# Routing cut in two: early token tiles are placed and gathered before the last tile is through its LayerNorm

## Chip, cores and metric

One core of one Trainium2 chip runs the whole program. The metric is the device time of one execution in microseconds (us). Five engines appear: TensorE (PE: matmuls; its weight loads are PEld), VectorE (DVE), ScalarE (ACT), GpSimd (POOL), and SyncE (SP), whose queue issues most transfers between HBM and the on-chip memory (SBUF).

## What is computed

A two-layer encoder on 512 tokens of width 1024. Layer 0 mixes tokens with a state-space part and gated linear attention, layer 1 with windowed attention; both end in a 1024x1024 output projection. Then a LayerNorm, a mixture of experts and a second LayerNorm:

```python
h = layer_norm(DEEPNORM_ALPHA * h + y, ln_mix_g[layer], ln_mix_b[layer])
y = hier_moe(h, ...)
h = layer_norm(DEEPNORM_ALPHA * h + y, ln_ffn_g[layer], ln_ffn_b[layer])

# hier_moe: xt is h as 512 rows
gp = softmax(xt @ w_group + b_group)              # 4 groups
grp = argmax(gp); p_grp = gp[tok, grp]
el = (xt @ w_router + b_router)[tok, grp]         # the 8 experts of that group
top_l, top_i = top_k(el, 2)
gate = softmax(top_l) * p_grp
# each of the two experts e of a token adds
#   gate * ((silu(x @ w1[e]) * (x @ w3[e])) @ w2[e])
```

There are 32 experts; w1 and w3 are 1024x512, w2 is 512x1024, all fp32.

## The kernel before

**Projection.** The 512 tokens are four tiles of 128. `out_part` makes one of four parts of a tile's output projection, each as three products (high and low halves of both operands). A tile is 48 matmuls of 512 columns; tile 3, the last, has 24 of 512 and 48 of 256 columns, which are as many columns in all. In layer 0 `out_proj` goes tile by tile: `operand(t)` transposes the mixer's output (tile `cat`) and splits it into `xh`, `xl`, four parts follow, and after them the tile's LayerNorm: `ln_stats` (L1067 to L1071; the power L1071 runs on POOL) and `ln_tile`, on DVE, with a row that multiplies by g (L1082) and a row that adds b (L1083), in two halves for tile 3. In layer 1 the same functions are called from `mixer1`, in an order written out by hand (`STEPS1`).

**Routing.** For each tile `route_tile` transposes x (L132, `ident`), copies it to `rxT` on ACT, multiplies it by the router's weights `wr` into the logits, and splits x into `xh` (ACT; DVE for tile 3) and `xl` (POOL, L1277). `logits` then adds the bias (L1282), and `route` does the rest for all four tiles at once: some 25 small DVE operations choose the group and the two experts, as a 0/1 matrix `ohb`; matmuls of `ohb` with the matrices `before` and `ones` give every token's place in its expert's list (`pos`); `select` compares it with a row of numbers to make the selection matrices `S`; `sort` ranks the experts by load (`eidx`, `erow`, `cap`); gates are worked out on DVE and POOL; `overflow_jobs` lists what doesn't fit; `gather` multiplies S by `xh` and `xl` (64 matmuls of 256 columns, 16 for a tile) and gives `xe`, the tokens in the experts' order; `arrange` brings places and gates into that order (`ppos`, `gT`, `gh`). Small matmuls called `warm` lie between, on the values as they come.

**Rounds.** `rounds` runs 13 rounds over the experts. `up` multiplies `xe` by w1 and w3, `turn` transposes, `down` multiplies by w2. SP streams weights into buffers of 2 MB (pools of 2, 2 and 3). Rounds 0 and 1 take fixed experts and are loaded ahead; later rounds are loaded by `eidx` (L1208).

**Who sets the order.** Inside `manual_schedule` PE keeps the order of the program; POOL's order follows the program everywhere; the rest is a scheduler's. Round 0 begins with the PE row `b<-w,xe` at L118.

Of the kernel before, what the change touches and what calls it, by code (L numbers as in the profile page):

```python
# [39 lines left out]
def row_bcast(ap1d, n, parts=128, off=0):  # L40
# [25 lines left out]
LP = 3  # L66

# [40 lines left out]
class Net:  # L108
# [862 lines left out]
    def mixer0_out(self, cat):  # L971
# [27 lines left out]
        def operand(t):  # L999
            for j in range(2):  # L1000
                b = self.bank()
# [44 lines left out]
    def out_proj(self, operand, hi, lo, split, layer, then, pre):  # L1046
# [4 lines left out]
        for t in range(4):  # L1051
            c = operand(t)
            for q in range(4):
                self.out_part(t, q, *c, hi, lo)
            self.ln_stats(t)
            self.ln_tile(t, gb)
            if t:
                then(t - 1)
        then(3)

    def ln_stats(self, t):
# [3 lines left out]
        if t == 3:  # L1065
            self.warm(st[:, 2, 0:1])
        V.bn_aggr(mv[:, 0:2], st.rearrange("p a b -> p (a b)"))  # L1067
        if t == 3:
            self.warm(mv[:, 0:1])
        V.tensor_scalar(mv[:, 2:3], mv[:, 1:2], 1e-5, None, op0=OP.add)  # L1070
        G.tensor_tensor(mv[:, 2:3], mv[:, 2:3], self.neghalf[:, 0:1], op=OP.pow)  # L1071
        if t == 3:
            self.warm(mv[:, 2:3])
# [178 lines left out]
    def route_tile(self, t):  # L1252

        nc = self.nc
        if t == 0:
            self.lgb = self.bank("l")
        V, S, G = nc.vector, nc.scalar, nc.gpsimd
        xT = []
        for j in range(2):
            b = self.bank("p")  # L1260
# [5 lines left out]
            if t == 3 and j == 0:  # L1266
                self.warm(x4[:, 0:1], 128)
            xT += [x4[:, 128 * k:128 * k + 128] for k in range(4)]
        hv = self.xh[:, t].rearrange("p k q -> p q k")
        if t == 3:  # L1270
            V.tensor_copy(hv, self.x[:, t].rearrange("p (q k) -> p q k", k=8))
        else:
            S.activation(hv, self.x[:, t].rearrange("p (q k) -> p q k", k=8), AF.Copy)
        lg = self.lgb[:, 36 * t:36 * t + 36]
        for k in range(8):
            self.mm(lg, xT[k], self.wr[:, k], k == 0, k == 7)
# [3 lines left out]
    def logits(self):  # L1280
        self.lg = self.M.tile([128, 4, 36], F32, name="lg", tag="lg")
        self.nc.vector.tensor_tensor(self.lg, self.lgb[:, 0:144].rearrange("p (t e) -> p t e", t=4),  # L1282
                                     self.br[:, None, :].to_broadcast([128, 4, 36]), op=OP.add)

    def route(self, layer):
        nc, M = self.nc, self.M
        V, S, G = nc.vector, nc.scalar, nc.gpsimd
# [4 lines left out]
        def rt(shape, name, dt=F32):  # L1292
            return M.tile([128] + shape, dt, name=name, tag=name)

        def bc(v, n):
            return v[:, :, None].to_broadcast([128, 4, n])
        lg = self.lg
        Gl, El = lg[:, :, 0:4], lg[:, :, 4:36]
        sm = rt([11, 4], "sm")
        gm, sg, pg, m1, m2, d21, den, g1, g2, kx, k2 = (sm[:, j] for j in range(11))  # L1300
        w4 = rt([3, 4, 4], "w4")
        ex, eq, ohg = (w4[:, j] for j in range(3))
        w8 = M.tile([128, 8, 4, 8], F32, name="w8", tag="hs", bufs=1)
        EM, key, oh1, oh2 = (w8[:, j] for j in range(4))
        w32 = w8[:, 4:8].rearrange("p a b e -> p (a b e)").rearrange("p (t g e) -> p t g e", t=4, g=4)
        gate = self.gate = rt([4, 32], "gate")

        def groups(v):

            return v[:, :, None].to_broadcast([128, 4, 4, 8]), ohg[:, :, :, None].to_broadcast([128, 4, 4, 8])  # L1310
        V.tensor_reduce(gm, Gl, axis=AX.X, op=OP.max)
        tt(eq, Gl, bc(gm, 4), OP.is_equal)
        tt(ex, Gl, bc(gm, 4), OP.subtract)
        tt(eq, eq, self.desc[:, None, 0:4].to_broadcast([128, 4, 4]), OP.mult)
        S.activation(ex, ex, AF.Exp)
        V.tensor_reduce(kx, eq, axis=AX.X, op=OP.max)
        tt(ohg, eq, bc(kx, 4), OP.is_equal)
        self.warm(gm[:, 0:1])
        self.warm(kx[:, 0:1])

        tt(w32, El.rearrange("p t (g e) -> p t g e", g=4), groups(EM)[1], OP.mult)
        V.tensor_reduce(EM, w32.rearrange("p t g e -> p t e g"), axis=AX.X, op=OP.add)
# [12 lines left out]
        tt(ohb.rearrange("p t (g e) -> p t g e", g=4), *groups(key), OP.mult)
        tt(d21, m2, m1, OP.subtract)

        b = self.bank()
        for t in range(4):
            o = b[:, 32 * t:32 * t + 32]  # L1340
            self.mm(o, self.before, ohb[:, t], True, t == 0)
            for s in range(t):
                self.mm(o, self.ones, ohb[:, s], False, s == t - 1)
        for t in range(4):
            self.mm(b[:, 128:160], self.ones, ohb[:, t], t == 0, t == 3)
        S.activation(d21, d21, AF.Exp)
        pos = self.pos = rt([4, 32], "pos")
        V.scalar_tensor_tensor(pos, b[:, 0:128].rearrange("p (t e) -> p t e", t=4), 1.0, ohb, op0=OP.add, op1=OP.mult)
        pb = self.bank()
        for t in range(4):  # L1350
            self.tp(pb[0:32, 128 * t:128 * t + 128], pos[:, t])
        self.posT = rt([512], "posT", BF)
        G.memset(self.posT, 0.0)
        cnt = self.cnt
        Sg = self.select(0, pos)
        V.tensor_scalar(self.posT[0:32], pb[0:32], 129.0, None, op0=OP.min)
        S.activation(cnt, b[:, 128:160], AF.Copy)
        self.sort(cnt)

        V.tensor_reduce(sg, ex, axis=AX.X, op=OP.add)  # L1360
# [5 lines left out]
        G.tensor_tensor(oh1, oh1, bc(g1, 8), op=OP.mult)  # L1366
        G.tensor_tensor(oh2, oh2, bc(g2, 8), op=OP.mult)
        G.tensor_tensor(oh1, oh1, oh2, op=OP.add)
        G.tensor_tensor(gate.rearrange("p t (g e) -> p t g e", g=4), *groups(oh1), op=OP.mult)
        self.overflow_jobs(layer, cnt)  # L1370
        xe = self.gather(0, Sg)
        self.arrange()
        if layer == 0:
            self.load_router(1)
        return xe, Sg

    def sort(self, cnt):
# [19 lines left out]
        b = self.bank()  # L1397
# [11 lines left out]

    def arrange(self):  # L1410
# [7 lines left out]
        b = self.bank()  # L1418
        for t in range(4):
            self.tp(b[0:32, 128 * t:128 * t + 128], self.gate[:, t])  # L1420
        gT = M.tile([128, 512], F32, name="gT", tag="GT", bufs=1)
        nc.scalar.activation(gT[0:32], b[0:32], AF.Copy)
        b = self.bank()
        for t in range(4):
            self.mm(b[:, 32 * t:32 * t + 32], gT[0:32, 128 * t:128 * t + 128], self.eone[0:32])
# [3 lines left out]
        nc.vector.tensor_tensor(self.gh[:, :, :, 1], bv, self.gh[:, :, :, 0].bitcast(F32), op=OP.subtract)  # L1429

    def select(self, g, pos=None):

        S = self.M.tile([128, 4, 256], F32R, name="S", tag="S", bufs=1)
        pos = self.ppos if pos is None else pos
        for kind, gr, q, p0 in ROUNDS:
# [4 lines left out]
            while a < len(ns):  # L1440
                m = sum(n == ns[a] for n in ns)
                d, o = [128, 4, m, ns[a]], 128 * q + sum(ns[:a])
                self.nc.vector.tensor_tensor(
                    S[:, :, o:o + m * ns[a]].rearrange("p t (a s) -> p t a s", a=m),
                    self.iota64[:, 0:ns[a]][:, None, None].to_broadcast(d),
                    pos[:, :, p0 + a:p0 + a + m][:, :, :, None].to_broadcast(d), op=OP.is_equal)
# [55 lines left out]
    def up(self, xe, q, ws, kind, between):  # L1502
# [3 lines left out]
        for b, nm in ((b1, "w1"), (b3, "w3")):  # L1506
            for k in range(8):
                for a, o, n in tiles(kind):
                    self.mm(b[o:o + n], xe[:, k, 128 * q + o:128 * q + o + n], ws[nm](a, k), k == 0, k == 7)
            if nm == "w1":  # L1510
# [59 lines left out]
    def moe(self, layer, then):  # L1570

        nx, S = self.route(layer)
        with self.tc.manual_schedule(engines={mybir.EngineType.PE}):
            parts = self.rounds(layer, nx, S)
# [519 lines left out]
```

## Time and profile before

| | us |
|---|---|
| median of 3 runs | 1565.31 |
| lowest and highest | 1565.18, 1565.65 |
| the profiled execution | 1567.3 |
| its span in the trace | 1565.5 |
| PE busy | 1395.2 (89%) |
| DVE busy | 672.0 (43%) |
| ACT busy | 370.4 (24%) |
| POOL busy | 138.6 (9%) |
| mean granted PE clock | 0.945 |

The span is what the trace covers of one execution; the 1.8 us between span and execution lie around it. Busy shares are means over a program with very different stages: two mixers, two routings (about 299 to 367 us and 1040 to 1081 us) and two runs of 13 rounds. PE streams matmuls one into the next, so the distance between two starts tells what one costs; the duration in a row also has its filling.

### The profile page before, as it was taken

The page shows a single profiled execution, that of the slowest core. Times are in us where ns is not written, and L with a number is a line of the kernel's source. Part 1 is how long each engine was busy: PE and PEld are TensorE (multiplying, and loading weights), DVE is VectorE, ACT ScalarE, POOL GpSimd, SP SyncE. Part 2 cuts the span into 40 slices and gives each one's busy share as a digit, 9 for nine tenths or more (in the row PEclk, how much of TensorE's full clock was granted, in tenths as well). Part 3 has the DMA queues.
Part 4 walks back from the last instruction along what each step waited for, and adds up shares of the span by engine and source line. Part 5 has one row for each costly group of instructions (what it writes and reads, how often), then busy time and mean ns, then how long its engine had stood idle before and what let it go on. Part 6 is the DMA issues. An engine that isn't in the chain of part 4 may idle for free. (4 is left out here: it accounts for less than half of the span.)

```text
span 1565.5 us, 21114 instructions
## 1 busy us (share of the span) xinstructions
PE 1395.2 (89%) x8299; PEld 817.3 (52%) x8299; DVE 672.0 (43%) x1467; ACT 370.4 (24%) x683; POOL 138.6 (9%) x120
## 2 busy tenths in 40 slices
PE   7998869989989999969797998998988999979885
PEld 6987656775525454324245865665434453424242
DVE  7989796462221332212127477663222223212125
ACT  3244735211101011001014565531101111101012
POOL 0000004230000000000005343021000000000003
PEclk9999889989999999999898999998999999999898
DMA  6233128365999999999995145475999999999993
GB/s 176 82 95 61 43 34 289 133 244 195 407 409 424 419 421 422 420 419 421 420 399 185 31 122 147 145 270 226 404 405 420 426 419 421 421 420 421 420 412 119
DMA packets 105879, 460.56 MB, mean 294 GB/s; under 512 B 17706, under 2 KB 43786, under 8 KB 63152
## 3 DMA queue, kind: packets, MB, share of 16 engines
q1 hardware_dynamic: 105664, 459.06, 75.0%
q8 instruction: 67, 1.10, 0.3%
q14 instruction: 36, 0.29, 0.1%
q0 software_dynamic: 112, 0.10, 0.0%
HBM read 454.41 MB, written 4.72 MB: 293 GB/s over the span
## 5 line engine op out<-in xcount | busy, mean ns | idle before, releaser
L118 PE MATMUL b<-w,xe 128*64 128x512 f32 (+1 forms) x2144 | 401.0, 618 | 37.9 <-DMA w<-in_moe_w_dram 34.5
L118 PEld LDWEIGHTS b<-w,xe 128*64 128x64 f32 (+1 forms) x2144 | 118.5, 127 | 289.5 <-issue 221.2
L118 PE MATMUL b<-w,hT 128*64 128x512 f32 (+1 forms) x1088 | 217.5, 629 | 33.8 <-DMA w<-in_moe_w_dram 30.9
L1567 DVE TENSOR_TENSOR x<-x,b 128x512 f32<-128x512 f32 x176 | 112.3, 682 | 156.5 <-PE b L118 154.2
L118 PEld LDWEIGHTS b<-w,hT 128*64 128x64 f32 (+1 forms) x1088 | 63.3, 129 | 173.7 <-issue 98.9
L1537 DVE SCALAR_TENSOR_TENSOR yl<-b,gs,yh 128x512 fp32r<-128x512 f32 x52 | 39.0, 751 | 215.2 <-ACT yh L1536 214.7
L118 PE MATMUL b<-S,xh 128*128 128x256 f32 x448 | 113.2, 293 | 0.0
L118 PE MATMUL b<-S,xl 128*128 128x256 f32 x448 | 111.5, 289 | 0.0
L1514 DVE TENSOR_TENSOR hs<-hs,b 128x512 f32<-128x512 f32 x26 | 17.9, 688 | 206.1 <-PE b L118 206.1
L118 PEld LDWEIGHTS b<-S,xh 128*128 128x128 f32 x448 | 88.7, 198 | 10.0 <-issue 9.9
L1536 ACT ACTIVATE yh<-b,gs 128x512 fp32r<-128x512 f32 x52 | 35.8, 688 | 234.2 <-PE b L118 233.9
L118 PE MATMUL b<-yh,GT 128*128 128x512 f32 x208 | 89.1, 432 | 0.1
L118 PEld LDWEIGHTS b<-S,xl 128*128 128x128 f32 x448 | 88.8, 198 | 0.0
L1100 POOL TENSOR_SCALAR lnmv<-lnmv 128x1 f32<-128x1 f32 x8 | 3.2, 398 | 963.9 <-DVE x L1099 483.9
L1522 ACT ACTIVATE hT<-b 128x512 f32<-128x512 f32 x26 | 15.6, 599 | 303.4 <-PE b L132 303.4
L118 PE MATMUL b<-yl,GT 128*128 128x512 f32 x208 | 81.9, 399 | 3.0 <-DVE yl L1537 3.0
L1513 ACT ACTIVATE hs<-b 128x512 f32<-128x512 f32 x26 | 15.6, 599 | 205.4 <-PE b L118 205.4
L118 PEld LDWEIGHTS b<-yh,GT 128*128 128x128 f32 x208 | 39.5, 190 | 46.3 <-issue 33.0
L118 PE MATMUL b<-wh,xt 128*128 128x256 f32 x384 | 54.6, 294 | 1.5 <-ACT wh L167 1.5
L1467 ACT ACTIVATE xe<-b 128x512 f32<-128x512 f32 (+1 forms) x56 | 31.7, 567 | 88.2 <-PE b L118 88.2
L118 PE MATMUL b<-xTh,spa 128*128 128x512 f32 x160 | 51.6, 394 | 0.5 <-ACT scv L1842 0.5
L118 PEld LDWEIGHTS b<-wh,xt 128*128 128x128 f32 x384 | 50.3, 199 | 2.7 <-ACT wh L167 1.9
(411 smaller groups left out, 2078.0 us busy)
## 6 DMA issues: line engine op xcount, KB each, us to landing
w<-in_moe_w_dram SPq DMA_DIRECT2D x288, 1024.0 KB, 19.8
w<-in_moe_w_dram SPq DMA_DIRECT2D x46, 2048.0 KB, 21.7
bias<-Ld SPq DMA_DIRECT2D x32, 384.0 KB, 3.5
wr<-in_ab_w_in_dram SPq DMA_DIRECT2D x8, 1024.0 KB, 5.8
x<-in_x_dram SPq DMA_DIRECT2D x8, 512.0 KB, 7.2
wo<-in_ab_w_out_dram SPq DMA_DIRECT2D x2, 2048.0 KB, 16.0
cw<-in_c_w_in_dram SPq DMA_DIRECT2D x2, 2048.0 KB, 11.4
cwo<-in_c_w_out_dram SPq DMA_DIRECT2D x16, 256.0 KB, 4.4
```

The costliest lines, as they stand in the source:

```text
L118: self.nc.tensor.matmul(o, l, r, start=start, stop=stop)
L1100: G.tensor_scalar(mv[:, 3:4], mv[:, 0:1], mv[:, 1:2], -1.0 / 1024, op0=OP.add, op1=OP.mult)
L1467: nc.scalar.activation(xe[:, 2 * kk:2 * kk + 2, 0:n], b.rearrange("p (j s) -> p j s", j=2)[:, :, 0:n], AF.Copy)
L1513: nc.scalar.activation(hs, b1, AF.Silu)
L1514: nc.vector.tensor_mul(hs, hs, b3)
L1522: self.nc.scalar.activation(hT, b.rearrange("p (k s) -> p k s", k=4), AF.Copy)
L1536: nc.scalar.activation(yh[:, j], b[j], AF.Copy, scale=gs)
L1537: nc.vector.scalar_tensor_tensor(yl[:, j], b[j], gs, yh[:, j].bitcast(F32), op0=OP.mult, op1=OP.subtract)
L1567: V.tensor_add(xs, xs, b)
```

## The change

- `route_tile` becomes `route_turn` (transposes, `rxT`, `xh`, now on ACT for every tile, and `xl`) and `route_logits`.
- `route` becomes `choose(a, z)`, `places(a, z)` and `gather_part(a, z)`, each for tiles a to z. With `CUT = 2, 3` layer 0 does tiles 0 and 1 first and layer 1 tiles 0 to 2; the rest comes after the last tile's logits. The sums of the two gathers stay in the same PSUM banks.
- `warm` goes from these places. `route_rest` has 16 matmuls of 512 columns that only fill (or start the banks at zero) while the last LayerNorm runs, and 6 more after the first gather.
- `sort`, `gates`, `overflow_jobs`, `gate_rows`, `pos_rows`, `arrange` and `slot_gates` go into round 0, behind parts of `up`.
- Layer 0's projection uses PSUM banks by tags (2, 2, 1, 2, 1) in place of eight free ones. In layer 1 the last three parts of the projection move from `STEPS1` into `mixer1_end`, in PE's written order, and `ln_mix`'s g and b are loaded a second time, into `w_yh`'s and `w_yl`'s places.

```diff
+CUT = 2, 3
+FILL, FILL2 = 3, 6
@@ def out_proj
-            if t:
-                then(t - 1)
-        then(3)
+            if t:
+                self.route_turn(t - 1)
+                self.route_logits(t - 1)
+        c = operand(3)
+        self.route_open()
+        with self.tc.manual_schedule(engines={mybir.EngineType.PE}):
+            if CUT[0] < 3:
+                self.choose(0, CUT[0])
+            self.out_part(3, 0, *c, hi, lo)
+            self.out_part(3, 1, *c, hi, lo)
+            self.route_turn(2)
+            self.out_part(3, 2, *c, hi, lo)
+            self.route_logits(2)
...
+            self.out_part(3, 3, *c, hi, lo)
+            self.route_rest(CUT[0], gb)
+
+    def route_rest(self, n, gb):
+
+        self.ln_stats(3)
+        self.ln_tile(3, gb)
+        self.gb0 = [self.bank("stst"[j]) for j in range(4)]
+
+        for _ in range(FILL):
+            for b in self.gb0:
+                self.mm(b, self.ones, self.posT)
+        for b in self.gb0:
+            self.mm(b, self.ones, self.posT, True, False)
+        self.route_turn(3)
+        self.places(0, n)
+        self.route_logits(3)
+        self.gather_part(0, n)
+        o = self.bank("o")
+        for _ in range(FILL2):
+            self.mm(o, self.ones, self.posT)
+        self.choose(n, 4)
+        self.places(n, 4)
+        self.gather_part(n, 4)
@@ def rounds
             def between():
                 steps(4)
+                if pr == 0:
+                    self.sort(self.cnt)
+                    self.gates()
+                    self.overflow_jobs(self.cnt)
+                    self.gate_rows()
                 GT.append(self.slot_rows(pr))
-            h = self.up(xe, q, W, kind, between)
+            h = self.up(xe, q, W, kind, between, self.pos_rows if pr == 0 else None)
+            if pr == 0:
+                self.arrange()
+            steps(2)
+            h = self.turn(h)
             if pr == 0:
                 gs = self.slot_gates(0, S)
-            steps(2)
-            h = self.turn(h)
@@ end of mixer1
+    def mixer1_end(self, hi, lo):
+
+        gb = self.load_gb("ln_mix", 1, self.rp, ("yh", "yl"))
+        self.load_round(1, 0)
+        self.route_open()
+        with self.tc.manual_schedule(engines={mybir.EngineType.PE}):
+            n = CUT[1]
+            self.route_turn(2)
+            self.out_part(3, 1, self.xh[:, 3], self.xl[:, 3], hi, lo)
+            self.route_logits(2)
+            self.choose(0, n)
+            self.out_part(3, 2, self.xh[:, 3], self.xl[:, 3], hi, lo)
+            self.out_part(3, 3, self.xh[:, 3], self.xl[:, 3], hi, lo)
+            self.route_rest(n, gb)
```

`order` rows below name a line, an instruction and its tiles; the changed kernel's L120 and L134 are L118 and L132 of before. First PE in layer 0, in the projection of tile 2 (`hi` and `lo` are the weights' halves), before:

```order
L118 MATMUL b_2893<-wr,rxT_2906 128x36 x4
L118 MATMUL b_2932<-hi_2693,xh 128x512
L118 MATMUL b_2959<-hi_2697,xh 128x512
L132 MATMUL b_2991<-ident,x 128x128 x4
L132 MATMUL b_2998<-ident,x 128x128 x4
L132 MATMUL b_3015<-ident,cat_1442 128x128 x4
L118 MATMUL b_2932<-hi_2693,xl 128x512
L118 MATMUL b_2932<-lo_2694,xh 128x512
```

and in the change, where this projection ends:

```order
L120 MATMUL b_2959<-lo_2698,xh 128x512
L134 MATMUL b_2991<-ident,x 128x128 x4
L134 MATMUL b_2998<-ident,x 128x128 x4
L134 MATMUL b_3015<-ident,cat_1442 128x128 x4
L134 MATMUL b_3022<-ident,cat_1443 128x128 x4
L120 MATMUL b_2893<-wr,rxT_2996 128x36 x4
```

The transposes of tile 1's x (`ident,x`) stood after the second matmul of tile 2's projection and now stand behind its last.

DVE in the LayerNorm of tile 1 at the same place, before:

```order
L1082 SCALAR_TENSOR_TENSOR x<-x,lnmv,ln_mix_g 128x1024
L1083 SCALAR_TENSOR_TENSOR x<-x,lnmv,ln_mix_b 128x1024
L1007 TENSOR_TENSOR xl<-b_2918,xh 128x512
L1007 TENSOR_TENSOR xl<-b_2925,xh 128x512
```

and in the change:

```order
L1114 SCALAR_TENSOR_TENSOR x<-x,lnmv,ln_mix_g 128x1024
L1009 TENSOR_TENSOR xl<-b_2918,xh 128x512
L1009 TENSOR_TENSOR xl<-b_2925,xh 128x512
L1115 SCALAR_TENSOR_TENSOR x<-x,lnmv,ln_mix_b 128x1024
```

The two halves of tile 2's `xl` moved ahead of the row that adds b.

PE at the start of round 0 in layer 0, in the change (before, the rows on `gate`, `gT` and `erow,posT` stood ahead of the first `w_0_0_0`):

```order
L120 MATMUL b_3362<-w_0_0_0_2729,xe_3038 64x512 x8
L134 MATMUL b_3372<-ident,pos 32x128 x4
L120 MATMUL b_3362<-w_0_0_1_2731,xe_3038 64x512 x8
L120 LDWEIGHTS rb
L120 MATMUL b_3399<-erow,rb 128x32
L120 LDWEIGHTS rb
L120 MATMUL b_3399<-identb,rb 128x32
L134 MATMUL b_3436<-ident,gate 32x128 x4
L120 LDWEIGHTS identb
L120 MATMUL b_3443<-posT,identb 64x512
```

The transposes of `pos` and `gate` and the matmuls of `sort` now lie between the products of w1.

## Rows read from the trace of the kernel before

**Rows 1.** Windows: span, its us; busy PE, PEld, DVE, ACT, POOL; PE clock; DMA share; GB/s.

```profile
371.00:825.00 454.00, 413.46 (x2326) 182.51 (x2324) 108.10 (x191) 49.20 (x77) 0.00 (x0) 0.98 1.01 414
...
352.00:371.00 19.00, 16.59 (x104) 13.31 (x106) 4.77 (x27) 3.27 (x6) 0.00 (x0) 0.82 0.04 5
...
388.00:390.00 2.00, 2.00 (x14) 0.59 (x10) 0.24 (x1) 0.00 (x0) 0.00 (x0) 1.00 0.66 238
```

**Rows 2.** Timeline (start, us, engine, line, count, [idle before]), round 0: PE and SP.

```profile
366.61 7.09 PE L118 MATMUL b<-w,xe 128*64 128x512 f32 x32
...
370.30 3.81 SPq L1222 DMA_DIRECT2D w<-in_moe_w_dram  x2
...
1081.38 7.09 PE L118 MATMUL b<-w,xe 128*64 128x512 f32 x32
```

**Rows 3.** Timeline of PE, layer 0, projections of tiles 2 and 3.

```profile
298.91 0.71 PE L118 MATMUL b<-hi,xh 128*128 128x512 f32 x2
302.63 1.97 PE L132 MATMUL b<-ident,x 128*128 128x128 f32 x8 [3.01 <-DVE x L1083]
...
317.20 1.87 PE L118 MATMUL b<-wr,rxT 128*128 128x36 f32 x16
...
319.30 0.47 PE L118 MATMUL b<-hi,xh 128*128 128x512 f32 x1
...
330.50 0.28 PE L118 MATMUL b<-lo,xh 128*128 128x256 f32 x1
```

**Rows 4.** Timeline of DVE and POOL, layer 0's LayerNorm rows.

```profile
287.79 1.28 DVE L1083 SCALAR_TENSOR_TENSOR x<-x,lnmv,ln_mix_b 128x1024 f32<-128x1024 f32 x1 [0.44 <-POOL lnmv L1071]
...
298.62 2.88 POOL L1277 TENSOR_TENSOR xl<-x,xh 128x1024 fp32r<-128x1024 f32 x1
...
298.69 3.89 DVE L1083 SCALAR_TENSOR_TENSOR x<-x,lnmv,ln_mix_b 128x1024 f32<-128x1024 f32 x1 [0.46 <-POOL lnmv L1071]
...
333.40 4.02 DVE L1083 SCALAR_TENSOR_TENSOR x<-x,lnmv,ln_mix_b 128x512 f32<-128x512 f32 x2
```

**Rows 5.** Timeline of ACT, DVE and PE, layer 0, from operands to round 0.

```profile
302.67 2.00 ACT L1273 ACTIVATE xh<-x 128x1024 fp32r<-128x1024 f32 x1 [3.72 <-DVE x L1083]
...
334.52 1.08 ACT L1265 ACTIVATE rxT<-b 128x512 f32<-128x512 f32 x2 [7.53 <-PE b L132]
...
343.87 0.31 DVE L1282 TENSOR_TENSOR lg<-b,br 128x144 f32<-128x144 f32 x1 [5.12 <-PE b L118]
...
349.08 0.29 DVE L1290 TENSOR_TENSOR ohb<-w,w 128x128 bf16<-128x128 f32 x1
...
350.53 1.29 DVE L1443 TENSOR_TENSOR S<-iota,pos 128x512 fp32r<-128x512 f32 x2
...
353.69 0.20 PE L118 MATMUL b<-erow,rb 32*128 32x32 bf16 x1 [2.52 <-DVE erow L1393]
...
354.44 0.41 PE L118 MATMUL b<-S,xh 128*128 128x256 f32 x1
...
359.35 0.41 PE L118 MATMUL b<-S,xl 128*128 128x256 f32 x1
...
360.09 0.28 PE L118 MATMUL b<-S,xh 128*128 128x256 f32 x1
...
364.17 0.27 PE L118 MATMUL b<-erow,posT 128*128 128x32 bf16 x4
...
365.60 1.07 PE L118 MATMUL b<-eone,gT 32*128 32x32 f32 x8 [0.73 <-ACT gT L1422]
```

**Rows 6.** Timeline of PE and DVE, layer 1, last parts of tile 3 and its LayerNorm.

```profile
1040.49 0.61 PE L118 MATMUL b<-chi,xh 128*128 128x512 f32 x2 [0.69 <-ACT xh L1961]
...
1047.91 0.28 PE L118 MATMUL b<-clo,xh 128*128 128x256 f32 x1
...
1050.81 4.00 DVE L1083 SCALAR_TENSOR_TENSOR x<-x,lnmv,ln_mix_b 128x512 f32<-128x512 f32 x2
```

**Rows 7.** Timeline of SP, layer 1: the weight load issued last before tile 3's parts.

```profile
1029.71 1.41 SPq L1222 DMA_DIRECT2D w<-in_moe_w_dram  x1
```

More of the change, by code (lines that the diff above doesn't have):

```diff
@@ L1044, in out_part, with out_proj @@
             V.bn_stats(self.lnst[:, t, j + (r if last else 0)], xs)
-    def out_proj(self, operand, hi, lo, split, layer, then, pre):
+    def out_proj(self, operand, hi, lo, split, layer, pre):
         split()
@@ L1050, in out_proj @@
         pre()
-        for t in range(4):
+        for t in range(3):
             c = operand(t)
@@ L1265, in route_tile @@
             S.activation(x4, b, AF.Copy)
-            if t == 3 and j == 0:
-                self.warm(x4[:, 0:1], 128)
-            xT += [x4[:, 128 * k:128 * k + 128] for k in range(4)]
+            self.rxT += [x4[:, 128 * k:128 * k + 128] for k in range(4)]
         hv = self.xh[:, t].rearrange("p k q -> p q k")
[L1270 to L1273, printed above, removed]
+        S.activation(hv, self.x[:, t].rearrange("p (q k) -> p q k", k=8), AF.Copy)
@@ L1280, in logits, with route_tile @@
[L1280 to L1287, printed above, removed]
+            self.mm(lg, self.rxT[k], self.wr[:, k], k == 0, k == 7)
+    def route_tile(self, t):
+        self.route_turn(t)
+        self.route_logits(t)
@@ new lines, in route_open, with rt @@
+    def route_open(self):
+        M = self.M
+        def rt(shape, name, dt=F32, **kw):
+            return M.tile([128] + shape, dt, name=name, tag=kw.pop("tag", name), **kw)
+        self.lg = rt([4, 36], "lg")
+        self.sm = rt([11, 4], "sm")
+        self.w4 = rt([3, 4, 4], "w4")
+        self.w8 = rt([8, 4, 8], "w8", tag="hs", bufs=1)
+        self.gate = rt([4, 32], "gate")
+        self.pos = rt([4, 32], "pos")
+        self.posT = rt([512], "posT", BF)
+        self.nc.gpsimd.memset(self.posT, 0.0)
+        self.S0 = rt([4, 256], "S", F32R, tag="S", bufs=1)
+        self.xe0 = self.half("xe0", [8, 256])
+        self.gb0 = []
@@ L1301, in route, with bc @@
[L1301 to L1310, printed above, removed]
+        def bc(v, m):
+            return v[:, :, None].to_broadcast([128, n, m])
@@ L1338, in route, with pos_rows @@
+    def pos_rows(self):
         b = self.bank()
         for t in range(4):
[L1340 to L1360, printed above, removed]
+            self.tp(b[0:32, 128 * t:128 * t + 128], self.pos[:, t])
@@ new lines, in pos_rows, with gates, tt @@
+        self.nc.vector.tensor_scalar(self.posT[0:32], b[0:32], 129.0, None, op0=OP.min)
+    def gates(self):
+        V, G = self.nc.vector, self.nc.gpsimd
+        def tt(o, x, y, op):
+            V.tensor_tensor(o, x, y, op=op)
+        gm, sg, pg, m1, m2, d21, den, g1, g2, kx, k2 = (self.sm[:, j] for j in range(11))
+        oh1, oh2 = (self.w8[:, j] for j in (2, 3))
+        bc = lambda v: v[:, :, None].to_broadcast([128, 4, 8])
+        V.tensor_reduce(sg, self.w4[:, 0], axis=AX.X, op=OP.add)
@@ L1365, in route, with gather_part @@
         tt(g2, g1, d21, OP.mult)
-        G.tensor_tensor(oh1, oh1, bc(g1, 8), op=OP.mult)
-        G.tensor_tensor(oh2, oh2, bc(g2, 8), op=OP.mult)
+        G.tensor_tensor(oh1, oh1, bc(g1), op=OP.mult)
+        G.tensor_tensor(oh2, oh2, bc(g2), op=OP.mult)
         G.tensor_tensor(oh1, oh1, oh2, op=OP.add)
[L1369 to L1375, printed above, removed]
+        G.tensor_tensor(self.gate.rearrange("p t (g e) -> p t g e", g=4), *self.groups(oh1), op=OP.mult)
+    def gather_part(self, a, z):
+        for t in range(a, z):
+            for k in range(8):
+                o = self.gb0[k // 2][:, 256 * (k % 2):256 * (k % 2) + 256]
+                self.mm(o, self.xh[:, t, k], self.S0[:, t], False, False)
+                self.mm(o, self.xl[:, t, k], self.S0[:, t], False, t == 3 and k % 2 == 1)
+                if t == 3 and k % 2:
+                    self.nc.scalar.activation(self.xe0[:, k - 1:k + 1], self.gb0[k // 2].rearrange("p (j s) -> p j s", j=2),
+                                              AF.Copy)
     def sort(self, cnt):
@@ L1500, in slot_rows, with up @@
         return GT
-    def up(self, xe, q, ws, kind, between):
+    def up(self, xe, q, ws, kind, between, within=None):
         nc = self.nc
@@ L1570, in moe @@
     def moe(self, layer, then):
-        nx, S = self.route(layer)
         with self.tc.manual_schedule(engines={mybir.EngineType.PE}):
-            parts = self.rounds(layer, nx, S)
+            parts = self.rounds(layer, self.xe0, self.S0)
+        if layer == 0:
+            self.load_router(1)
         with self.tc.issue_after(self.w2_dma.ins):
@@ L1619, in rounds, with overflow_jobs @@
         return parts
-    def overflow_jobs(self, layer, cnt):
+    def overflow_jobs(self, cnt):
         nc, M = self.nc, self.M
```

153 lines of the change are left out of this document (88 added, 65 removed), and 3 rows, old and new, of the table STEPS1.

## The prediction

> **What bounds the kernel now.** I read the windows first. Through the rounds of layer 0 (371 to 825 us) the DMA share is 1.01 at 414 GB/s while PE is busy 413 of 454 us: the stream of weights sets the pace [rows 1]. Just ahead, from 352 to 371, the DMA share is 0.04. So the rounds can't be shortened by what this change does, but they can be begun earlier. The timeline of PE and SP shows what begins them: round 0's first matmul starts at 366.61 in layer 0 and 1081.38 in layer 1, and the next weights are issued 3.7 us after the first, at 370.30, when w1's products have freed two buffers [rows 2]. The question for each layer is thus how much earlier round 0 starts, and what is added to round 0. The added work counts too: at 388 to 390 the stream has a gap again (share 0.66) [rows 1], because its next buffers wait for round 0's products, so PE still sets the pace there.
>
> The rest is two chains from projection to round 0, read row by row.
>
> **Layer 0, projection.** Tile 2's projection starts at 298.91. After two matmuls PE stands for 3.01 us because tile 1's x, which it is to transpose, isn't ready, and then works below full clock; it ends at 317.20 [rows 3], 18.3 us in all. Tile 3's projection, as many columns, takes from 319.30 to 330.78, that is 11.48 [rows 3]. In the change tile 1's transposes stand behind tile 2's projection, which then runs unbroken: 298.91 + 11.48 and 0.2 for its first products = 310.6. Behind it follow 8 transposes of x and 8 of the operand (1.0 each; the eight that were broken into took 1.97 below full clock [rows 3]) and the logits of tile 1, 1.87 [rows 3]: tile 3 starts at 314.5. Its own 11.48, with tile 2's transposes (1.0) and logits (1.87) woven in, ends at **328.9**, 1.9 before the old 330.8.
>
> **Layer 0, LayerNorm.** From the end of the projection to the last row on x (333.40 + 4.02 [rows 4]) it took 6.64. The row that adds b takes 1.28 when POOL is free and 3.89 when POOL's `xl` (2.88) runs beside it; that DVE row ended 1.1 us after POOL's [rows 4]. For tile 3 the two halves took 4.02 in the same way, where some 1.3 would be expected. In the change POOL's `xl` of tile 2 stands ahead of tile 3's power, and tile 2's x is ready long before, so nothing of POOL lies beside tile 3's rows: 6.64 - 2.6 = 4.0, x at 332.9. The bounds are 6.64 (the collision comes back) and 4.0. The 16 filling matmuls of 512 columns take 16 x 0.24 (twice the 0.12 below for 256 columns) = 3.8 at full clock and end within it.
> The Trainium skill says in "GPSIMD Engine Reference", section "8. Key points", that GpSimd shares its SBUF interfaces with VectorE and contends with DVE instructions that have two SBUF inputs; the row at 298.69 agrees, and by that rule the term is the same.
>
> **Layer 0, last logits and choice.** From x to the biased logits it took 6.4 (337.42 to 343.87 [rows 4, 5]). Now: `rxT` of the second half waits on ACT for `xh`, which moved there from DVE and takes 2.00; then 0.60 for that copy, half of 1.87 for the logits, and a few tenths for hand-overs [rows 3, 5]: I take 4.3, between 3.5 (the bare sum) and 6.4, nearest to the pieces since the small `warm` matmuls are gone. 337.2. The choice took 343.87 to 349.37, 5.5 [rows 5]. For two tiles the operations are as many and fixed costs rule them, so 5.5 again; POOL's `xl` of tile 3 now runs into it, for which I add 1.0 (bounds 0 and 2.6, the collision above): 343.7. Places and S took 2.45 after that (to 351.82 [rows 5]); for two tiles 2.0: 345.7. `sort` is no longer in the way, where PE waited 2.52 for `erow` [rows 5]. The last gather is 32 of 64 matmuls at 0.12 (34 starts from 360.09 to 364.17 [rows 5]) = 3.84; the first 32 and the 6 fillers lie beside the choice. Round 0 starts at **349.6** in place of 366.61, for `arrange` (364.17 to 366.61, 2.44 [rows 2, 5]) is also behind it now: **-17.0**.
>
> **Layer 1.** Here nothing is gained in the projection. PE went through tile 3's last parts from 1040.49 to 1048.19, 7.7 us [rows 6]. The logits of tile 2 (1.87) now stand between them, the parts are 72 pieces of 256 columns at 0.12 = 8.6, and I add 0.5 for the transposes: the end comes at 1051.5, **+3.3**. LayerNorm took 6.62 (to 1054.81 [rows 6]) with the same collision; 6.62 - 2.6 + 0.8, since tile 2's `xl` is now nearer = 4.8: 1056.3. Logits as above 4.3: 1060.6. The first gather is now 48 matmuls, 5.7, to 1066.3, and 6 fillers of 0.24 end at 1067.8, after the choice (1067.1). They and not the choice are late next here. Places and S 1.5, 16 matmuls 1.9: **1071.2** in place of 1081.38, **-10.2**.
>
> **Round 0.** `arrange`'s 2.44 and the four transposes of places (0.5) come into it, less the wait of 0.73 for `gT` [rows 5], which w3's products should cover: **+2.2** in each layer. Bounds: 0.5, if the stream and not PE sets round 0's pace after all (only the places' transposes lie ahead of the buffers that restart it), and 5, if each hand-over from DVE and POOL stops PE once more. `sort` and `gates` have 3.5 us of w1's products above them. Their late result, `eidx`, is first needed for the loads of round 2, which wait for round 1's buffers anyway: no cost. The second load of g and b adds 1 MB in layer 1, 2.5 us at 414 GB/s, ahead of an idle stream: no cost unless the gain there were above 10.
>
> **Sum.** -17.0 + 2.2 - 10.2 + 2.2 = -22.8. The profiled execution is 1567.3, so 1544.5; it lies 2.0 over the median of the runs, so the median becomes **1542.5**.
>
> **Rivals.**
> 1. *The clock falls and the gathers run at half of it.* In before the first 24 gather matmuls came every 0.2135 us (354.44 to 359.35), the later ones every 0.12 [rows 5], after PE had waited 2.52; the granted clock of that window is 0.82, a mix of the 1.2 and 2.4 GHz levels [rows 1]. The change leaves PE some 2 us without work while ACT copies `xh`. For it speaks that the wait of 3.01 was followed by slow transposes [rows 3]; against it the fillers. Price: layer 0's last 32 at 0.2135 cost +3.0; in layer 1 48 cost +4.5, the fillers +1.4, the last 16 +1.5. Together +10.4: **1552.9**. Half of it, when the clock comes back during the first gather, is as good as in my range. The Trainium skill, "TensorE: Matmul & The Clock Gate", section "What's actually happening", has the throttled state as the default, which activity releases; by it idle PE in these chains would bring this rival. The trace bears that out for the first gather of before.
> 2. *Round 0 hides what is moved into it.* The 1.01 share speaks for it, the gap at 388 against it [rows 1]. Then +0.5 in place of +2.2, 3.4 in all: **1539.1**.
> 3. *The change doesn't do what it says:* PE's written order in round 0 has `sort`'s matmuls and the transposes of `gate` among w1's and w3's products, so PE stands wherever DVE or POOL is late, and the tables cost there what they cost before. `sort` alone made PE wait 2.52, `gT` 0.73 [rows 5]; with the collisions of POOL and DVE on top, 5 to 11 in each layer is lost: **1553 to 1565**.
> 4. *Slower: layer 1's second load of g and b.* It stands on SP behind 5 MB of weights, the last of which is issued at 1029.71 [rows 7] and which take 12 us at 414 GB/s; it also waits for its place to be free. LayerNorm of tile 3 needs it at about 1053, so on paper it is early by some 8 us. Should the place be free only late, every weight behind it in the queue is late as well. It costs one for one from 1053 on and decides when it comes after 1053 + 22.8 = 1076; at 1083, **1572**. Nothing in the trace shows such a late reader, so the chance is small.
>
> **Chances.** Forecast 0.49, clock 0.30 (half or whole), round 0 hidden 0.11, not carried through 0.07, slower 0.03. The range 1537 to 1554 takes in the first three, with the collision terms' bounds; what is left out is most of rivals 3 and 4 and some mishap of the sum. A measurement of this kernel tells 0.2% (3.1 us) from nothing. Faster by more than that is the forecast, rivals 1 and 2 and most of 3: 0.92. Within it: the upper end of 3, 0.04. Slower 0.04.
>
> **What would show it.** Round 0's first matmul at 348 to 351 and at 1069 to 1073 (counted from the span's start); the projection of tile 2 in 11 to 12 us without a break; tile 3's two rows that add b at 0.7 each; gather starts 0.12 apart; the weights' stream restarting 4 us after round 0 starts. Gathers 0.21 apart mean rival 1. A distance between round 0 and round 1 that grew by under 1 means rival 2, by over 5 rival 3. A wait of DVE for `ln_mix` in layer 1 means rival 4. The sum is wrong if round 0 starts earlier by these amounts and the end doesn't follow.

## The result, and the profile after

The changed kernel takes **1543.2 us** (median of 4 runs, 1538.5 to 1547.2) where the kernel before, run beside it, takes 1565.5 (1565.2 to 1567.1): a ratio of 0.9854, 95% interval 0.9826 to 0.9883. Forecast were 1542.5, from 1537 to 1554. The same kernel in a second comparison gave 1540.7 and 0.9875 (0.9846 to 0.9905). Runs of one kernel differ by up to 1% there (before: 1553 to 1569), so stages are compared by their traces below.

The profiled execution of the changed kernel took 1547.2. First round 0 and the issue of weights behind it, the answer to [rows 2] (timeline, columns as there):

```profile
351.92 3.65 PE L120 MATMUL b<-w,xe 128*64 128x512 f32 x16 [0.72 <-ACT xe L1436]
...
355.62 4.50 SPq L1254 DMA_DIRECT2D w<-in_moe_w_dram  x2
...
1059.08 3.65 PE L120 MATMUL b<-w,xe 128*64 128x512 f32 x16 [0.72 <-ACT xe L1436]
```

Round 0 starts 14.7 us earlier in layer 0 and 22.3 earlier in layer 1, and the stream again restarts 3.7 after it. A wait shows that the prediction had not named: 0.72 for the last copy of `xe`.

The projections of layer 0, the answer to [rows 3], and the fillers behind them:

```profile
300.17 0.71 PE L120 MATMUL b<-hi,xh 128*128 128x512 f32 x2
...
311.20 1.04 PE L134 MATMUL b<-ident,x 128*128 128x128 f32 x8
...
314.65 0.47 PE L120 MATMUL b<-hi,xh 128*128 128x512 f32 x1
...
328.89 3.63 PE L120 MATMUL b<-posT,ones 128*128 128x512 bf16 x16
```

Tile 2's projection now takes 11.0 us without a break. Next DVE and POOL, the answer to [rows 4]:

```profile
299.88 1.28 DVE L1009 TENSOR_TENSOR xl<-b,xh 128x512 fp32r<-128x512 f32 x2
300.34 2.96 POOL L1301 TENSOR_TENSOR xl<-x,xh 128x1024 fp32r<-128x1024 f32 x1
301.07 3.31 DVE L1115 SCALAR_TENSOR_TENSOR x<-x,lnmv,ln_mix_b 128x1024 f32<-128x1024 f32 x1
...
331.66 1.41 DVE L1115 SCALAR_TENSOR_TENSOR x<-x,lnmv,ln_mix_b 128x512 f32<-128x512 f32 x2
...
335.74 2.86 POOL L1301 TENSOR_TENSOR xl<-x,xh 128x1024 fp32r<-128x1024 f32 x1 [4.25 <-ACT xh L1300]
```

Tile 3's two rows take 1.41 together in place of 4.02; tile 1's row is still held (3.31), but no longer stands ahead of tile 2's `xl`. Then the routing of layer 0, the answer to [rows 5], from ACT, DVE and PE:

```profile
333.71 1.96 ACT L1300 ACTIVATE xh<-x 128x1024 fp32r<-128x1024 f32 x1
335.47 0.62 ACT L1297 ACTIVATE rxT<-b 128x512 f32<-128x512 f32 x1
...
338.06 0.23 DVE L1338 TENSOR_TENSOR lg<-b,br 128x72 f32<-128x72 f32 x1 [3.16 <-PE b L120]
...
342.37 0.22 DVE L1338 TENSOR_TENSOR ohb<-w,w 128x64 bf16<-128x64 f32 x1
...
344.03 1.47 PE L120 MATMUL b<-posT,ones 128*128 128x512 bf16 x6
...
346.04 0.23 DVE L1397 SCALAR_TENSOR_TENSOR pos<-b,ohb 128x64 f32<-128x64 f32 x1 [3.37 <-ACT cnt L1396]
...
347.11 0.39 PE L120 MATMUL b<-S,xh 128*128 128x256 f32 x1 [1.34 <-DVE S L1508]
```

The choice is done at 342.6, but DVE waits 3.37 until PE has gone through the first gather and the 6 fillers. Of 61 regular steps between gather starts 24 are slow steps (0.21 us) and 37 are fast steps (0.12); all slow steps are in the first gather. Layer 1 has 16 slow steps and 45 fast steps.

For the comparisons four stretches are read from each profile: A, from layer 0's first projection product to the end of its last projection; B and C, from that end to round 0 in layers 0 and 1; D, from round 0's first matmul to the `w,hT` products of round 0 and of round 1.

| profile | A | B | C | D, layer 0 | D, layer 1 |
|---|---|---|---|---|---|
| before | 60.7 | 35.8 | 33.2 | 16.5, 42.2 | 16.5, 42.1 |
| after | 54.2 | 22.9 | 21.0 | 18.4, 45.8 | 18.4, 44.1 |
| after, run again | 54.2 | 22.9 | 21.0 | 18.4, 45.8 | 18.4, 44.1 |

In the first profile layer 0's projection began at 274.84, in the second at 270.48 (before: 270.06). That difference of 4.4 us is not the change's: the profiles of the changed kernel and its variants have that start anywhere from 268.4 to 276.6.

A begins with the first product, and the first product isn't the same place in both kernels. PE's first row of the projection, before and after, transposes the operands:

```profile
268.28 1.94 PE L132 MATMUL b<-ident,cat 128*128 128x128 f32 x8 [3.37 <-DVE cat L815]
...
271.62 3.47 PE L134 MATMUL b<-ident,cat 128*128 128x128 f32 x16 [3.28 <-DVE cat L817]
```

Before, 8 transposes (tile 0) stand ahead of the first product; in the change it is 16 (tiles 0 and 1). From the first transpose to the end of the projection it took 62.5 and now takes 57.4: of the 6.5 in A only 5.1 is gained.

### The profile page after: what moved, and what is told of

It reads as the page before. It is cut to its first block, busy times and chain, and to the rows that moved or that the text cites. A ratio compares the mean times of both kernels' runs of the same rounds, so it can differ in the third digit from the quotient of the medians.

```text
span 1545.4 us, 21171 instructions
## 1 busy us (share of the span) xinstructions
PE 1390.9 (90%) x8303; PEld 800.9 (52%) x8303; DVE 668.1 (43%) x1514; ACT 373.6 (24%) x689; POOL 137.1 (9%) x120
## 5 line engine op out<-in xcount | busy, mean ns | idle before, releaser
L120 PE MATMUL b<-w,xe 128*64 128x512 f32 (+1 forms) x2144 | 402.1, 620 | 38.9 <-DMA w<-in_moe_w_dram 34.0
L120 PEld LDWEIGHTS b<-w,xe 128*64 128x64 f32 (+1 forms) x2144 | 116.0, 127 | 291.9 <-issue 221.5
L120 PE MATMUL b<-w,hT 128*64 128x512 f32 (+1 forms) x1088 | 223.5, 643 | 30.3 <-DMA w<-in_moe_w_dram 28.7
L120 PEld LDWEIGHTS b<-w,hT 128*64 128x64 f32 (+1 forms) x1088 | 61.4, 131 | 177.8 <-issue 109.2
L120 PE MATMUL b<-S,xh 128*128 128x256 f32 x448 | 113.3, 293 | 2.4 <-DVE S L1508 2.4
L120 PE MATMUL b<-S,xl 128*128 128x256 f32 x448 | 111.4, 288 | 0.0
L120 PEld LDWEIGHTS b<-S,xh 128*128 128x128 f32 x448 | 88.6, 198 | 12.5 <-issue 9.9
L1603 ACT ACTIVATE yh<-b,gs 128x512 fp32r<-128x512 f32 x52 | 35.8, 688 | 238.5 <-PE b L120 238.3
L120 PE MATMUL b<-yh,GT 128*128 128x512 f32 x208 | 89.0, 432 | 0.1
L120 PEld LDWEIGHTS b<-S,xl 128*128 128x128 f32 x448 | 88.6, 198 | 0.0
L120 PE MATMUL b<-yl,GT 128*128 128x512 f32 x208 | 81.7, 398 | 1.9 <-DVE yl L1604 1.8
L120 PEld LDWEIGHTS b<-yh,GT 128*128 128x128 f32 x208 | 39.5, 190 | 46.9 <-issue 36.3
L120 PE MATMUL b<-wh,xt 128*128 128x256 f32 x384 | 55.3, 296 | 4.0 <-ACT wh L169 4.0
L120 PEld LDWEIGHTS b<-wh,xt 128*128 128x128 f32 x384 | 51.0, 201 | 5.4 <-ACT wh L169 4.6
L120 PE MATMUL b<-xTh,spa 128*128 128x512 f32 x160 | 51.6, 394 | 0.5 <-ACT scv L1917 0.5
L1549 DVE TENSOR_REDUCE gs<-b 64x1 f32<-64x2 f32 (+2 forms) x64 | 10.0, 157 | 83.8 <-PE b L120 82.0
## 6 DMA issues: line engine op xcount, KB each, us to landing
w<-in_moe_w_dram SPq DMA_DIRECT2D x46, 2048.0 KB, 21.6
```

The costliest lines, as they stand in the source:

```text
L120: self.nc.tensor.matmul(o, l, r, start=start, stop=stop)
L1549: nc.vector.tensor_reduce(gt[o:o + n], b[o:o + n, 2 * a:2 * a + 2], axis=AX.X, op=OP.add)
L1603: nc.scalar.activation(yh[:, j], b[j], AF.Copy, scale=gs)
```

## The experiments

**The change again.**

> The changed kernel once more, for comparison on the same chip. The sum and every rival that the first result left standing give the same: 22 us below the kernel before (1539 to 1547). If the first 300 us, which the change leaves alone, were only late by chance in the first profile (some 3.4 us), round 0 of layer 0 starts about 18 us earlier than before here (at 348 to 349 from the span's start); if they are late because of the change, it starts at 352 again.

Ratio 0.9875; round 0 started at 347.5, so the first profile's late start was chance. The stages took the same in both profiles (table above).

**No split.** `CUT = 0, 0`; with no early tiles, nothing is chosen or gathered ahead.

```diff
-CUT = 2, 3
+CUT = 0, 0
```

> All four tiles are chosen, placed and gathered in one piece after the last logits; everything else as in the change (reordered projection, fillers, tables in round 0). If the split is worth what the sum says (32 gather matmuls off the path in layer 0, 48 in layer 1, at 0.12 each, less some 1.3 and 3.9 that the first gather was late): slower than the change by 3 in layer 0 and 3 in layer 1, 5 to 8 in all. If the clock decides (nothing for PE to do during the choice but the 6 fillers, so the gather begins at 0.21 apart): 2 to 3 more in each layer, 10 to 14 in all. If the split is worth nothing, since the first gather made PE late: within 2 us of the change.

Ratio 0.9945 (0.9924 to 0.9965): 0.0070 or 11 us slower than the change. B is 27.1 and C 27.4, +4.3 and +6.5. PE timeline of layer 0:

```profile
338.09 0.21 PE L120 MATMUL b<-ohb,before 128*128 128x32 bf16 x2 [2.62 <-DVE ohb L1339]
...
340.59 0.58 PE L120 MATMUL b<-S,xh 128*128 128x256 f32 x1 [1.96 <-DVE S L1509]
...
344.39 0.41 PE L120 MATMUL b<-S,xl 128*128 128x256 f32 x1
```

After waits of 2.62 and 1.96 the gather begins 0.21 apart, now on the path: 17 and 23 slow steps at 0.09 more each take 1.6 and 2.1 of its time. The split is worth 11, in the 10 to 14 of the expectation for a deciding clock and not in the 5 to 8 of the sum. How much of the 11 is the clock stays open, since slow steps made PE late in the change too.

**Tables ahead of round 0.**

```diff
         self.places(n, 4)
+        self.pos_rows()
+        self.sort(self.cnt)
+        self.gates()
+        self.overflow_jobs(self.cnt)
         self.gather_part(n, 4)
...
+            self.gate_rows()
+            self.arrange()
             parts = self.rounds(layer, self.xe0, self.S0)
```

> The split stays, but sort, gates, jobs, places' transposes and the rows of gates are done ahead of round 0, as in the kernel before. Theory of the sum: round 0 starts 4 to 5 us later in each layer (sort in front of the last gather about 2, arrange 2.4), and round 0 itself is 2.2 shorter, so 2 to 3 slower in each layer, 4 to 6 in all. Rival (the stream hides what round 0 has to do in addition): only 0.5 is given back, 4 in each layer, 8 to 9 in all. If PE's written order in round 0 wastes as much as the tables cost outside: within 2 us of the change.

Ratio 0.9927 (0.9902 to 0.9952), 8 us slower. In the trace B is 28.6 and C 25.2, +5.7 and +4.3. PE, layer 0:

```profile
346.42 0.18 PE L120 MATMUL b<-erow,rb 32*128 32x32 bf16 x1 [1.99 <-DVE erow L1459]
...
354.22 1.07 PE L120 MATMUL b<-eone,gT 32*128 32x32 f32 x8 [0.72 <-ACT gT L1482]
...
355.42 7.09 PE L120 MATMUL b<-w,xe 128*64 128x512 f32 x32
```

The old waits for `erow` and `gT` are back, and round 0's D is 16.5 again in layer 0: 1.9 is given back. So the sum's +2.2 was near, and the stream does not hide it. Two parts of the loss are the clock's: behind the wait for `erow` 17 steps of layer 0's last gather were slow (1.5), and in layer 1 the clock fell as round 0 began (D 18.2, 1.7). By the traces 7.8 are lost in both layers together, 4.6 without these two, within the 4 to 6 of the sum; by the ratios 8.

**POOL's low half beside tile 3's rows.** `xl` of tile 2 is issued after tile 3's power.

```diff
         self.ln_stats(3)
+        self.low(2)
         self.ln_tile(3, gb)
```

> POOL makes the low half of tile 2's x after tile 3's power, as in the kernel before, so that it runs beside the rows that add b to tile 3. Theory: DVE's two rows take 4.0 in place of 1.4, and x of tile 3 is 2.6 later in each layer: 5 us slower than the change, round 0 of layer 0 2.6 later. Rival: the fillers and the copies on ACT hide it: under 2 us. If PE, idle for 2.6 more, also falls to the lower clock level in the gathers: 8 or more.

Ratio 0.9913 (0.9882 to 0.9943), 6 us slower, though the two intervals overlap. B 24.8 and C 24.0: +1.9 and +3.0. DVE and POOL, layer 0:

```profile
325.69 3.01 POOL L1307 TENSOR_TENSOR xl<-x,xh 128x1024 fp32r<-128x1024 f32 x1
...
325.89 4.01 DVE L1116 SCALAR_TENSOR_TENSOR x<-x,lnmv,ln_mix_b 128x512 f32<-128x512 f32 x2
```

1.41 became 4.01, as in [rows 4], in both layers: the term of 2.6 is shown by this edit alone. B grew by less, since the first gather had 16 slow steps in place of 24 (0.7).

**No second fill.** `FILL2 = 0`.

> The 6 fillers between the two gathers are left out (FILL2 = 0; they add nothing to the result). Theory that they only stand in the way, since the first gather already ends after the choice: the places' matmuls come 1.3 to 1.5 earlier in each layer, 3 us faster than the change (ratio to before 0.002 lower), last gather at 0.12 as before. Rival (they hold the clock): the last gather runs at 0.21, +3.0 in layer 0 and +1.5 in layer 1, so the sum is 1 to 2 slower.

B 21.6, C 19.7: 1.3 less each, and the last gather as fast (37 and 46 fast steps). Ratio 0.986 (0.9838 to 0.9881), which doesn't resolve 2.6 us. The 6 fillers hold nothing here and cost 1.3 in each layer.

**Copies first on ACT.** `xh` of tile 3 is issued after the second `rxT`.

```diff
+        with ExitStack() as es:
+            if t == 3:
+                es.enter_context(self.tc.issue_after(self.rxi.ins))
+            S.activation(hv, ...)
```

> On ACT the two copies of tile 3's transposed x come ahead of the copy to xh (2.0 us), which stood between them. Theory: from the end of the projection to the biased logits it takes 8.2 to 9.0 in the change; without the wait 1.7 to 1.9 less in each layer, 3.5 us faster in all. Rival: POOL's low half is then later and runs further into the choice, which the shared interface slows: of the 1.8 about 1 is given back, or all of it.

The logits came 1.7 and 0.9 earlier, but B is 22.5 and C 18.6. The choice took 7.0 and 6.2 in place of 4.5, and in layer 0 33 steps of the gather were slow, in layer 1 only 2. Ratio 0.987 (0.9849 to 0.9891): no gain to be seen; the rival was right for layer 0. In layer 1 C is 2.4 shorter; how much of that the clock gave was not settled.

**No first fill.** `FILL = 0`.

> The 12 plain fillers ahead of tile 3's transposes are left out (FILL = 0; the 4 that start the banks stay). If they hold the clock: tile 3's transposes, the last logits and the first gather run at the lower level throughout (64 gather starts 0.21 apart in place of 17 to 25 slow ones), 2 to 5 us in each layer, 4 to 10 slower in all. If the clock falls anyway a little later, as the 16 to 25 slow gather matmuls of the change suggest: within 2 us of it.

B 23.0, C 21.5 (+0.1, +0.5); 22 and 12 slow steps, no more than in the change. Ratio 0.985 (0.9824 to 0.9875). The granted clock shows what the fillers did. Windows (columns as in [rows 1]) from 0.6 us before tile 3's x is complete, over its transposes and the beginning of its logits, layers 0 and 1, in the change and then in this run:

```profile
332.40:336.00 3.60, 2.49 (x20) 1.99 (x19) 1.66 (x5) 2.79 (x3) 0.26 (x1) 1.00 1.03 387
1041.60:1045.20 3.60, 2.46 (x23) 2.02 (x22) 1.84 (x4) 2.88 (x3) 0.36 (x1) 1.00 1.04 387
...
329.20:332.80 3.60, 3.17 (x18) 2.89 (x18) 1.62 (x4) 2.56 (x3) 0.04 (x1) 0.54 1.02 384
1038.10:1041.70 3.60, 3.15 (x22) 2.83 (x22) 1.86 (x4) 2.88 (x3) 0.34 (x1) 0.69 1.05 389
```

With the fillers the clock was 1.00 there, without them 0.54 and 0.69, and the logits came 0.3 and 0.8 us later after x. So they hold the clock into the logits, but not through the gather, and nearly nothing of it reaches round 0.

**Woven order.** The last part's places stand inside the first gather.

```diff
-        self.gather_part(0, n)
...
-        self.choose(n, 4)
+        self.choose(n, 4)
+        self.gather_part(0, n - 1)
+        if n == 2:
+            self.gather_part(1, 2, range(4))
         self.places(n, 4)
+        self.gather_part(n - 1, n, range(4, 8) if n == 2 else range(8))
         self.gather_part(n, 4)
```

> PE's order changed: the places of the last part stand inside the first gather (after 24 of 32 matmuls in layer 0, after 32 of 48 in layer 1), the rest of the first gather covers the making of the last S, and the 6 fillers go. Theory that the first gather and the fillers made PE late for the last part by 3.4 to 4.6 (choice done at 338.1 and 1046.6 there, places read at 341.6 and 1051.1): round 0 starts 3 us earlier in each layer, 6 us faster than the change in all. Rival: with the clock at its lower level the first 24 to 32 matmuls already end after the choice, and only the fillers are gained: 2 to 3 us.

B 20.6, C 18.4: 2.2 and 2.5 less, ratio 0.9842 (0.9815 to 0.987), by itself not clear of the change's. The first 24 matmuls, slow, ended at 341.64, just after the choice: some of the 3 us stayed with the clock.

**Both edits.**

> Both edits that paid: the woven order of PE and tile 3's copies ahead of the copy to xh. Theory: from the end of the projection to round 0 it took 22.9 and 21.0 in the change, 20.6 and 18.4 woven; the copies take 1.7 and 0.9 more off where the gather isn't at the lower clock for longer: 19 and 17.5, 6 to 7 us faster than the change in all, a ratio to before of 0.983. Rival (the choice, slowed by POOL beside it, is now what PE waits for, as it took 6.1 in place of 4.4 in layer 1 of the run with the copies alone): no faster than woven.

B 21.5, C 18.5, ratio 0.9846 (0.9827 to 0.9866): no better than woven. DVE and POOL in layer 0 show why:

```profile
334.03 2.89 POOL L1304 TENSOR_TENSOR xl<-x,xh 128x1024 fp32r<-128x1024 f32 x1 [4.93 <-ACT xh L1303]
...
334.31 2.71 DVE L1341 TENSOR_TENSOR w<-lg,sm 128x8 f32<-128x8 f32 x2
```

Two operations on 8 columns take 2.71 us, until POOL ends at 336.9.

**Both edits without the first fill.**

> As the kernel with both edits, but without the 12 plain fillers ahead of tile 3's transposes. If they hold nothing (the run without them cost 0.2 and 0.5 us): the same within 1 us in layer 0 and 1 alike. If the shorter way makes the difference, because PE would reach the gather before the clock falls with fillers and after it without: 2 to 5 slower, more than half of the gather's starts 0.21 apart.

B 21.4, C 19.1, 23 and 20 slow steps, ratio 0.9847 (0.9829 to 0.9866): the same within the spread. The logits again came later (2.1 and 1.2 us), but POOL's `xl` then ran less into the choice, which took 5.3 and 5.0 in place of 7.0 and 6.2.

**Before, with tile 2's projection unbroken on PE.** `operand(2)`, its four parts and LayerNorm, `operand(3)` and then tile 1's routing, in PE's written order; nothing else.

> The kernel before with one change: tile 1's transposes and logits stand behind tile 2's projection on PE. Sum's mechanism alone: from tile 2's first product to the end of tile 3's projection 28 to 29 in place of 31.9, and all behind it as much earlier: 3 to 3.5 us faster, ratio 0.998. If the stall only moves (tile 2's operands or banks late next, or the LayerNorm of tile 2 then in the way of tile 3): within 1 us of before.

Ratio 1.0019 (1.0001 to 1.0037): no gain. PE and DVE, layer 0:

```profile
303.06 0.50 PE L118 MATMUL b<-hi,xl 128*128 128x512 f32 x1 [3.83 <-DVE xl L1007]
...
298.52 3.87 DVE L1096 SCALAR_TENSOR_TENSOR x<-x,lnmv,ln_mix_b 128x1024 f32<-128x1024 f32 x1 [0.45 <-POOL lnmv L1084]
302.32 1.28 DVE L1007 TENSOR_TENSOR xl<-b,xh 128x512 fp32r<-128x512 f32 x2
```

The stall moved: the projection's second matmul now waits 3.83 for tile 2's `xl`, which stands on DVE behind the row that POOL holds up. So PE's order alone gains nothing. The change has DVE's order changed as well, with tile 2's `xl` ahead of that row, and no such wait; DVE's order alone was not tried.

**Low half on DVE.** Both edits, and tile 3's `xl` on DVE right after the last S.

```diff
         self.places(n, 4)
+        with self.tc.issue_after(self.sel.ins):
+            self.low(3, self.nc.vector)
```

> The kernel with both edits, and the low half of tile 3's x is made on DVE, right after the last S, in place of POOL beside the choice. Theory that POOL's operation holds up one operation of the choice until it ends (2.6 us in place of 0.13, in both layers of the run with both edits): the choice takes 4.4 to 4.6 again in place of 6.0 to 6.8, the new DVE operation (some 1.4) lies beside the gather of the tile before; from the end of the projection to round 0 about 19.5 in layer 0 and 17 in layer 1 (21.5 and 18.5 with POOL), 8 to 10 us faster than the change in all, ratio to before 0.982 or lower. Rival (the last gather waits for the low half, or the clock takes the gain): 21 and 18, no better than woven.

B 20.0, C 17.5; median 1532.9 beside 1563.2, ratio **0.9803** (0.9774 to 0.9833). DVE, layer 0:

```profile
333.04 0.24 DVE L1349 TENSOR_TENSOR w<-lg,sm 128x8 f32<-128x8 f32 x2
...
338.96 1.97 DVE L1311 TENSOR_TENSOR xl<-x,xh 128x1024 fp32r<-128x1024 f32 x1
```

The pair of operations is back at 0.24, and the choice at 4.5 and 3.9. This is the fastest of the kernels: 8 to 11 us below the change by the ratios, and by B and C together 1.6 below the woven order and 2.6 below both edits; the ratio alone does not separate it from the woven order. B and C stayed 0.5 above the forecast, for the rival came in part: in layer 0 the last gather had 17 slow steps (1.5), and in layer 1, where only 3 steps were slow, the last gather waited 1.00 for the low half. PE, layer 1:

```profile
1043.39 0.38 PE L120 MATMUL b<-S,xl 128*128 128x256 f32 x1 [1.00 <-DVE xl L1311]
```

## Why the prediction was right, and where its steps were off

The mechanism was right: the stream follows round 0 at a constant 3.7 us, the gain is what is gained ahead of round 0, and the end follows (from layer 1's round 0 to the end it takes 484.1 before, 486.3 and 483.3 in the change's two profiles). That the sum came within 1 us is in part luck: its terms were off by up to 3 us each, both ways. The parts, forecast against the two profiles:

- **Layer 0's projection: forecast 1.9 earlier, measured 5.1 from the first transpose on.** Tile 2's own stretch was near: 11.7 forecast, 11.0 measured; from tile 2's first product to the end 30.0 forecast, 28.9 measured, where before took 31.9. The other 2.1 lie ahead of tile 2. Some of them are the clock's: before, the granted clock from 270 to 275 us was 0.57 and the first products came 0.43 apart; in the run of before with tile 2's projection unbroken, which has the same order up to there, only one did nearly so, and 1.2 of the 2.1 was gone. What moved tile 1's transposes ahead of the first product was not tried. And the step named PE's order as the cause: with that alone nothing is gained. DVE's order, shown ahead of the prediction but left out of the step, goes with it.
- **LayerNorm: forecast 4.0, measured 4.0** (329.05 to 333.07). The step on which the Trainium skill agreed, "GPSIMD Engine Reference", section "8. Key points", that GpSimd contends with DVE instructions that have two SBUF inputs, holds in the runs too: in the three places above where POOL's row stands beside DVE's (the change, the low half beside tile 3's rows, both edits) the DVE operation is held until POOL's ends.
- **Logits: forecast 4.3, measured 5.0** in layer 0 and 4.2 in layer 1. `rxT` waits for the copy to `xh` in both, as foreseen; the 0.8 more in layer 0 is the clock's: the second 8 products of the logits (`wr,rxT`) took 1.88 there and 1.08 in layer 1.
- **Choice: forecast 6.5, measured 4.5.** POOL's `xl` was nearly over when it began, so nothing was added; where `xl` was moved into it, it did cost 1.6 to 2.5. And "fixed costs rule them, so 5.5 again" was wrong: with POOL out of the way the choice took 5.5 for four tiles (before), 4.5 for two and 3.9 for one (low half on DVE, layers 0 and 1).
- **Last part: forecast to begin with the choice's end, measured 3.4 later, where some 0.8 passes when PE is free.** This is the term that failed: "the first 32 and the 6 fillers lie beside the choice" held only at 0.12 a matmul and with a choice of 6.5; 24 ran at 0.21, and the choice was done 2.0 sooner, so PE was late and nothing of these 2.0 came through. It is rival 1 in part: the clock fell in the first gather, not in the last, where it would have cost 3.0.
- **The copy of `xe`, put at nothing.** From the last gather's start to round 0 the sum has 3.84, measured are 4.8 (347.11 to 351.92), 0.72 of it PE's wait for the last copy. Before, `arrange` lay there. With these terms B came to 22.9 where the sum has 20.7.
- **Layer 1: projection forecast +3.3.** The parts themselves took 11.05 (1027.08 to 1038.13) in place of 7.70, as forecast. But from round 0 of layer 0 to their end the trace has +4.6, of which 3.7 arose in rounds 0 and 1 of layer 0, so only some +1.0; the mixer ahead of them was shorter by the rest, which no run explains. What remains of this stretch differs by up to 6 us between the variants' profiles, so the +1.0 is rough. **C: forecast 19.7, measured 21.0**, with the fillers late as said. Together -11.2, where -10.2 was forecast.
- **Round 0: forecast +2.2, measured +2.0** (D, 16.46 to 18.44) in each layer. Rival 2 falls: the round got longer by this, round 1's products came as much later, and with the tables outside it was short again. Rival 3 falls: PE shows no wait for `rb` or `gate` in round 0. Rival 4 falls: the second load of g was issued at 1022.65, long before the row that adds b in tile 3 at 1040.75, and DVE shows no wait for it.

Two of the signs were set badly. Round 0 of layer 0 was to begin at 348 to 351 and began at 351.92 and 347.51: the stretch ahead of the projection varies by more than this window. Round 0 of layer 1 was to begin at 1069 to 1073 and began at 1059.08 and 1054.78: the sign leaves out what layer 0 gains (17.0 - 2.2), with which it would be at 1056.4.

By the traces the parts come to -5.1 -12.9 +3.7 +1.0 -12.2 +2.0 = -23.5, and the fall of the clock below, 1.7, is within the 3.7. The median moved by 22, with an interval of 18 to 27. Not tried by themselves are the PSUM banks by tags and the absence of `warm`.

## What to carry to other kernels

When a stage behind is bound by a stream that starts with its first matmul, every microsecond ahead of that matmul counts in full, and tables that are first needed later belong behind it. Filling an idle engine isn't free: check that what fills ends before what is waited for, at the slower of the two speeds that the trace shows (the 6 fillers cost 1.3 us in each layer). And look for the operation that holds up another engine's: moving one POOL operation to DVE took 2.6 us off the two routings, where the first set of fillers was worth 0.6 at most.

## What was not expected of the hardware

The clock also fell in the middle of round 0, where PE had no idle time. Windows of the changed kernel's second profile (columns as in [rows 1]) and the products that begin in them:

```profile
362.00:367.00 5.00, 5.00 (x34) 3.17 (x32) 2.41 (x8) 0.89 (x2) 0.00 (x0) 0.91 1.03 439
367.00:372.00 5.00, 5.00 (x20) 1.46 (x18) 0.69 (x2) 0.65 (x1) 0.00 (x0) 0.75 0.31 129
```

```profile
365.95 8.78 PE L120 MATMUL b<-w,hT 128*64 128x512 f32 x32
```

The granted clock was 0.91 and 0.75, a mix of the 2.4 and 1.2 GHz levels, and 32 products took 8.78 us where the same row takes 7.09 in layer 1 of that profile. Ahead of it PE had gone through small matmuls (transposes, products of 4 and 32 columns). The same rows stand in the run with POOL's low half beside, and there the clock stayed at 1.00. Of the eleven profiles that have the tables in round 0 (the change, twice, and its variants but one) five show this fall, each in one of the two layers, at 1.7 us each time. What decides it was not settled.
The rule of "TensorE: Matmul & The Clock Gate" in the Trainium skill, section "What's actually happening", that activity releases the throttle, is borne out in part: the first gather rose to full speed as it went on in the change's two profiles, and behind the fillers the clock stayed at 1.00 for tile 3's transposes, where it was down without them; but they did not spare the gather its slow start, and in round 0 the clock fell while PE was busy throughout.
